# A two-block transformer forward pass: the low part of streamed weights made by an accumulating DMA instead of a GpSimd subtraction

## Chip, cores, metric

One NeuronCore of a Trainium2 chip runs the whole program in one launch. The metric is device microseconds of one execution. Times are compared as the median of several runs.

## What is computed

The reference chains two blocks in float32 over 512 tokens of width 1024. Only the first block is touched by the change:

```
h = x
h = h + token_mixer(rmsnorm(h))           # w_in (two attentions: top-k "A", differential "B"), w_out
h = h + cross_attention(rmsnorm(h), mem)  # w_xk, w_xv on 256 memory rows; w_xq, w_xo
h = h + conv_glu(rmsnorm(h))              # w_ffn_in, w_ffn_out
...
second_block(h)                           # gated recurrence, latent attention, merge, norm
```

Every `x @ w` is done to more than single-pass precision: an operand is written as a high part (rounded to the matmul's own format, fp32r) plus a low part (operand minus high part), and a product is three matmuls, high by high, high by low and low by high.

## The kernel before

**Weights.** A weight chunk is streamed from DRAM in pieces of 128 partitions by 1024 columns (512 KB). `W(src, nk, ncol)` (line 178) takes one buffer of the ring `WH` (high parts) and one of the ring `WL` (low parts) per piece, four buffers each, and calls `split` (line 167). `split` takes a raw buffer `WR` (ring of three), loads the piece with a DMA on SyncE's queue (line 169), writes the high part (line 173 on GpSimd, POOL, or line 175 on ScalarE, ACT) and subtracts it from the raw piece for the low part (line 176, on VectorE, DVE, or on POOL). A chunk of 8 k-tiles by 256 columns is two pieces, so the four buffers hold two chunks: one in use by TensorE (PE), one being prepared.

**Who does which part** is set by `setw`: the modes are taken in turn, the first letter naming the engine of the high part (`a` ACT, `p` POOL), the second that of the low part (`d` DVE, `p` POOL). From line 767 to line 1127 the mode is `"ap"`: ACT rounds, POOL subtracts. That stretch has 56 pieces: 16 of `w_inc` (projections of the token mixer), 8 each of `w_xk`, `w_xv`, `w_out`, `w_xq`, `w_xo`. It is the stretch from about 24 to 445 us of the span. Before it only the first projection (`w_in0`) is streamed, after it come the feed-forward part and the second block.

**Stages of that stretch.** Up to about 124 us PE runs the projections; DVE and POOL apply norms and rotary tables to their results (lines 392 to 430, 550) and DVE runs the index scores (line 808) and the top-k of attention A (lines 819, 822). From 124 to 200 us the first half of the differential attention runs (`soft`: line 609 maxima on DVE, line 617 exponentials on ACT). From 200 to 305 us its second half, attention A and the projections of the memory (lines 941 to 979) share the engines. From 305 us on, `residual_lin` (`w_out`), the query projections and cross-attention, and `w_xo` follow, with PE busy almost without a break.

**Order.** The program is written as interleaved generators (`pipeline`); a scheduler then sets the order of the instructions on each engine and each engine runs its own queue strictly in that order. An instruction that waits holds everything behind it on its engine. `mm3` (lines 218 to 220) issues the three matmuls of a product.

Of the kernel before, what the change touches and what calls it, by code (L numbers as in the profile page):

```python
# [14 lines left out]
AF = mybir.ActivationFunctionType  # L15
OP = mybir.AluOpType
# [46 lines left out]
def _body(nc, tc, ctx, d):  # L63
    TT = nc.vector.tensor_tensor
    TS = nc.vector.tensor_scalar
    STT = nc.vector.scalar_tensor_tensor
    ACT = nc.scalar.activation
    PTT = nc.gpsimd.tensor_tensor
# [43 lines left out]
    def rr(ap):  # L112
        return ap.bitcast(F32R)
# [7 lines left out]
    def f32(ap):  # L121
        return ap.bitcast(F32)
# [40 lines left out]
    def setw(*m):  # L163

        wmode[:], wturn[0] = m, 0

    def split(src, h, l, raw=None):
        raw = wr_()[:, :src.shape[-1]] if raw is None else raw
        nc.sync.dma_start(raw, src)
        m = wmode[wturn[0] % len(wmode)]  # L170
        wturn[0] += 1
        if m[0] == "p":
            PTS(h, raw, 1.0, 0.0, op0=OP.mult, op1=OP.add)  # L173
        else:
            ACT(h, raw, AF.Copy)  # L175
        (TT if m[1] == "d" else PTT)(l, raw, f32(h), op=OP.subtract)  # L176

    class W:


        def __init__(self, src, nk, ncol):
            self.per = 1024 // ncol
            self.hi, self.lo = [], []
            for k0 in range(0, nk, self.per):
                n = (min(nk, k0 + self.per) - k0) * ncol
                h, l = wh_(F32R)[:, :n], wl_(F32R)[:, :n]
                split(src[:, k0 * ncol:k0 * ncol + n], h, l)
                self.hi.append(r3(h, ncol))
                self.lo.append(r3(l, ncol))
# [20 lines left out]
    def steps(g, last):  # L210

        for st_ in g:
            if st_ == last:
                return True
        return False
# [110 lines left out]
    for k in range(KD):  # L326
        if k:
            nc.sync.dma_start(xs[k], d["xT"][:, k * T:(k + 1) * T])
        if k == 1:
            nc.scalar.dma_start(pos, d["pos"])  # L330
        if k % 2 == 0:
            raw, h, l = wr_(), wh_(F32R), wl_(F32R)
        c_ = slice((k % 2) * N0, (k % 2 + 1) * N0)
        split(d["w_in0"][:, k * N0:(k + 1) * N0], h[:, c_], l[:, c_], raw[:, c_])
        w0.append((h[:, c_], l[:, c_]))
        hilo(X.hk(k), X.lk(k), xs[k], v_("g_mix", k), pool=k % 2 == 1)
        st.add(xs[k])
# [426 lines left out]
    st0["tab_kk"] = kk  # L764
    st0["tab_i"] = (kk[0][:, :, 1:2], kk[1][:, :, 1:2])
    steps(proj, "end")
    setw("ap")
    steps(proj, "end")
    st0["tab_kb"] = rope_table([3], 1, tabs[2][:, :256], tabs[2][:, 256:])
    st0["tab_qb"] = rope_table([2], 1, tabs[3][:, :256], tabs[3][:, 256:])  # L770
# [83 lines left out]
    drain(proj)  # L854


    setw("ap")
    Oa = Act(4, R[0:1], R[1:2])
    banks(2, 2, 2, 2)
    poA, poB = Ring(pout.t[0:1]), Ring(pout.t[1:2])  # L860
# [870 lines left out]
    for q in range(4):  # L1731
        next(ma)
        h, l = (rr(t[q // 2][:, (q % 2) * 1024:(q % 2) * 1024 + 1024]) for t in (R[8:10], R[10:12]))
        split(d["w_o2"][0][:, q * 1024:(q + 1) * 1024], h, l)
        wo_hi += [h[:, 0:512], h[:, 512:1024]]
        wo_lo += [l[:, 0:512], l[:, 512:1024]]
# [3 lines left out]
    for n in range(NT):  # L1740
        s_ = slice(n * P, n * P + P)
        x = [xr(), xr()]
# [105 lines left out]
```

## Time and profile before

| | us |
|---|---|
| median of three runs | 1481.96 (1481.84 to 1483.73) |
| the profiled execution | 1483.48 |
| its span, first to last instruction | 1481.70 |
| PE busy | 1433.6 (97% of the span) |
| DVE busy | 967.2 (65%) |
| ACT busy | 571.5 (39%) |
| POOL busy | 504.2 (34%) |

Busy times are unions of the records on an engine. Issuing a DMA is not counted as busy. The ends of matmuls are modelled, so a busy PE is not PE at its peak. The granted clock is that of TensorE, 1.00 being 2.4 GHz and 0.50 being 1.2 GHz. A gap is put down to the semaphore that came last.

### The profile page before, as it was taken

What the parts mean: (1) busy time and instruction counts of PE and PEld (TensorE: products, weight loads), DVE (VectorE), ACT (ScalarE), POOL (GpSimd) and SP (SyncE); (2) the same over time, 40 slices, a digit from 0 to 9 for tenths busy, and PEclk for the clock granted to TensorE, in tenths of its full rate; (3) what the DMA queues carried; (4) which work ended last, traced back from release to release, by engine and by line L of the source; (5) the groups of instructions that cost most, each with busy time, mean ns of one, the idle gap of its engine ahead of it and who ended that gap; (6) DMA issues with size and microseconds to landing.
All of it is one profiled execution on the core that took longest, in us unless ns stands there. A gap on an engine that the chain in (4) does not pass through costs nothing.

```text
span 1481.7 us, 21172 instructions
## 1 busy us (share of the span) xinstructions
PE 1433.6 (97%) x7920; PEld 1240.7 (84%) x7920; DVE 967.2 (65%) x1908; ACT 571.5 (39%) x1136; POOL 504.2 (34%) x455
## 2 busy tenths in 40 slices
PE   6989899999999999999999999999999999998998
PEld 5988899888878788888888988888888898977887
DVE  8899898654445776356665556655448777886553
ACT  4535767744542222112223345344323333342121
POOL 6665677445531332332321111121114222331110
PEclk9999989999999999999999999999999999999999
DMA  6121143233212222333223422222332223235522
GB/s 213 59 72 58 44 143 123 92 108 134 72 58 86 100 89 76 98 122 100 87 78 106 129 90 92 86 93 82 133 110 79 100 97 111 79 121 189 196 78 86
DMA packets 54039, 150.59 MB, mean 102 GB/s; under 512 B 6064, under 2 KB 11696, under 8 KB 53936
## 3 DMA queue, kind: packets, MB, share of 16 engines
q1 hardware_dynamic: 53792, 149.24, 30.5%
q8 instruction: 62, 1.02, 0.3%
q14 instruction: 41, 0.34, 0.1%
q10 hardware_dynamic: 144, 0.00, 0.0%
HBM read 134.54 MB, written 14.68 MB: 101 GB/s over the span
## 4 chain that ended last, share of the span: by engine, by line
PE 81%; DVE 9%; issue 4%; ACT 2%; DMA 2%; POOL 1%; SPq 0%; POOLq 0%; DVEq 0%; ACTq 0%
PE PS L218 19%; PE PS L219 18%; PE PS L220 18%; PE PT L218 7%; PE PT L219 7%; PE PT L220 7%; PE PS L437 2%; DVE R L155 1%; PE PS L1400 1%; DVE WL L176 1%; DVE S L822 1%; DVE S L808 1%; PE PS L876 1%; DVE keep L819 0%; DMA S<-kv_d 0%
## 5 line engine op out<-in xcount | busy, mean ns | idle before, releaser
L218 PE MATMUL PS<-R,WH 128*128 128x512 f32 x920 | 359.1, 392 | 1.8 <-DVE S L1156 1.0
L219 PE MATMUL PS<-R,WH 128*128 128x512 f32 x920 | 359.5, 391 | 0.2 <-DVE R L155 0.2
L220 PE MATMUL PS<-R,WL 128*128 128x512 f32 x920 | 358.4, 391 | 0.0
L176 DVE TENSOR_TENSOR WL<-WR,WH 128x1024 fp32r<-128x1024 f32 (+4 forms) x176 | 209.7, 1194 | 110.2 <-ACT WH L175 91.2
L175 ACT ACTIVATE WH<-WR 128x1024 fp32r<-128x1024 f32 (+2 forms) x144 | 150.1, 1044 | 220.6 <-PE PS L219 151.6
L173 POOL TENSOR_SCALAR WH<-WR 128x1024 fp32r<-128x1024 f32 (+3 forms) x88 | 89.0, 1011 | 370.1 <-PE PS L219 145.6
L218 PEld LDWEIGHTS PS<-R,WH 128*128 128x128 f32 x920 | 172.5, 188 | 37.8 <-DVE S L1156 1.5
L220 PEld LDWEIGHTS PS<-R,WL 128*128 128x128 f32 x920 | 173.0, 188 | 35.7
L219 PEld LDWEIGHTS PS<-R,WH 128*128 128x128 f32 x920 | 173.1, 188 | 34.8 <-DVE R L155 0.5
L218 PE MATMUL PS<-WH,R 128*128 128x256 f32 (+2 forms) x568 | 166.8, 299 | 7.4 <-POOL WH L173 5.5
L220 PE MATMUL PS<-WH,R 128*128 128x256 f32 (+2 forms) x568 | 168.1, 297 | 1.5 <-DVE R L152 1.5
L176 POOL TENSOR_TENSOR WL<-WR,WH 128x1024 fp32r<-128x1024 f32 x56 | 139.5, 2500 | 86.7 <-ACT WH L175 77.9
L219 PE MATMUL PS<-WL,R 128*128 128x256 f32 (+2 forms) x568 | 166.7, 295 | 0.9 <-DVE WL L176 0.9
L218 PE MATMUL PT<-R,WH 128*128 128x512 f32 x352 | 140.4, 399 | 4.6 <-DVE S L1706 3.6
L219 PE MATMUL PT<-R,WH 128*128 128x512 f32 x352 | 139.7, 397 | 1.7 <-DVE R L155 1.7
L220 PE MATMUL PT<-R,WL 128*128 128x512 f32 x352 | 139.4, 396 | 0.0
L218 PEld LDWEIGHTS PS<-WH,R 128*128 128x128 f32 x568 | 111.6, 197 | 10.7 <-POOL WH L173 5.5
L220 PEld LDWEIGHTS PS<-WH,R 128*128 128x128 f32 x568 | 111.1, 196 | 4.6 <-DVE R L152 1.9
L219 PEld LDWEIGHTS PS<-WL,R 128*128 128x128 f32 x568 | 110.8, 195 | 4.6 <-DVE WL L176 2.3
L218 PEld LDWEIGHTS PT<-R,WH 128*128 128x128 f32 x352 | 67.4, 192 | 19.1 <-DVE S L1706 3.9
L219 PEld LDWEIGHTS PT<-R,WH 128*128 128x128 f32 x352 | 67.1, 191 | 15.5 <-DVE R L155 2.3
L220 PEld LDWEIGHTS PT<-R,WL 128*128 128x128 f32 x352 | 67.3, 191 | 14.3
(395 smaller groups left out, 2641.2 us busy)
## 6 DMA issues: line engine op xcount, KB each, us to landing
WR<-w_fi_d SPq DMA_DIRECT2D x44, 512.0 KB, 3.6
WR<-w_inc_d SPq DMA_DIRECT2D x16, 512.0 KB, 3.6
WR<-w_fo_d SPq DMA_DIRECT2D x16, 512.0 KB, 3.7
WR<-w_gl_d SPq DMA_DIRECT2D x16, 512.0 KB, 3.2
WR<-w_xk_d SPq DMA_DIRECT2D x8, 512.0 KB, 3.6
WR<-w_xv_d SPq DMA_DIRECT2D x8, 512.0 KB, 3.6
WR<-w_out_d SPq DMA_DIRECT2D x8, 512.0 KB, 3.6
WR<-w_xq_d SPq DMA_DIRECT2D x8, 512.0 KB, 3.6
```

The costliest lines, as they stand in the source:

```text
L155: TT(ol, src, f32(oh), op=OP.subtract)
L173: PTS(h, raw, 1.0, 0.0, op0=OP.mult, op1=OP.add)
L175: ACT(h, raw, AF.Copy)
L176: (TT if m[1] == "d" else PTT)(l, raw, f32(h), op=OP.subtract)
L218: nc.tensor.matmul(ps, sh, mh, start=first, stop=False)
L219: nc.tensor.matmul(ps, sh, ml, start=False, stop=False)
L220: nc.tensor.matmul(ps, sl, mh, start=False, stop=last)
L437: nc.tensor.transpose(out, in_, ident)
L808: STT(sc[b], rl, wi[:, b, h:h + 1], sc[b], op0=OP.mult, op1=OP.add)
L822: nc.vector.match_replace(sc[b], m8, sc[b], TAKEN)
L876: nc.tensor.matmul(ps, qa[g][:, q2 * 2 + hh, b * P:(b + 1) * P], rr(ka[j])[:, :N], start=j == 0, stop=j == 1)
L1400: nc.tensor.matmul(ps, qp[hh][:, s_], rr(kpe[j])[:, :N], start=False, stop=j == 1)
```

## The change

Mode `"ap"` becomes `"ax"` in both places. In this mode ACT writes the high part as before; ACT also writes minus the high part into the low-part buffer (the raw piece times -1, rounded to the same format); then a DMA on GpSimd's queue loads the same piece from DRAM a second time and adds it to what is in the buffer, which leaves raw minus high part there. The GpSimd subtraction is gone. All lines behind line 176 move down by five.

```diff
-        (TT if m[1] == "d" else PTT)(l, raw, f32(h), op=OP.subtract)
+        if m[1] == "x":
+
+            ACT(l, raw, AF.Copy, scale=-1.0)
+            nc.gpsimd.dma_start(l, src, accum_op=OP.add)
+        else:
+            (TT if m[1] == "d" else PTT)(l, raw, f32(h), op=OP.subtract)
...
-    setw("ap")
+    setw("ax")
...
-    setw("ap")
+    setw("ax")
```

The instructions of the engines move with it, since the scheduler orders them anew. Three places:

POOL's queue where the first pieces of `w_inc` are prepared (about 25 us), before. Names are out<-in, with buffer numbers:

```order
L151 TENSOR_SCALAR R_62<-S_96,vec 128x512
L176 TENSOR_TENSOR WL_105<-WR_99,WH_101 128x1024
L176 TENSOR_TENSOR WL_106<-WR_100,WH_102 128x1024
L176 TENSOR_TENSOR WL_107<-WR_98,WH_103 128x1024
L415 TENSOR_TENSOR S_82<-S_96,S_90 128x2x32
L416 TENSOR_TENSOR S_82<-S_96,S_90 128x2x32
```

The same place in the changed kernel:

```order
L151 TENSOR_SCALAR R_62<-S_96,vec 128x512
L179 DMA WL_105<-w_inc_d 128x1024
L179 DMA WL_106<-w_inc_d 128x1024
L179 DMA WL_107<-w_inc_d 128x1024
L420 TENSOR_TENSOR S_82<-S_96,S_90 128x2x32
L421 TENSOR_TENSOR S_82<-S_96,S_90 128x2x32
```

Three subtractions that read two buffers have become three DMA issues at the same place of the queue.

ACT's queue at the same time, before:

```order
L365 ACTIVATE S_83<-S_84 128x4x32
L175 ACTIVATE WH_101<-WR_99 128x1024
L175 ACTIVATE WH_102<-WR_100 128x1024
L175 ACTIVATE WH_103<-WR_98 128x1024
L490 ACTIVATE S_96<-PS_114 128x452
```

and in the changed kernel:

```order
L370 ACTIVATE S_83<-S_84 128x4x32
L175 ACTIVATE WH_101<-WR_99 128x1024
L178 ACTIVATE WL_105<-WR_99 128x1024
L175 ACTIVATE WH_102<-WR_100 128x1024
L178 ACTIVATE WL_106<-WR_100 128x1024
L178 ACTIVATE WL_107<-WR_98 128x1024
L175 ACTIVATE WH_103<-WR_98 128x1024
L495 ACTIVATE S_96<-PS_114 128x452
```

Each rounding has a second ACT instruction of the same shape beside it, from the third piece on ahead of it.

ACT's queue in the stretch from 200 us on, where the memory's key and value weights are prepared between exponentials (L617), before:

```order
L175 ACTIVATE WH_102<-WR_98 128x1024
L960 ACTIVATE S_90<-PS_110,SMALL 128x256 x2
L175 ACTIVATE WH_103<-WR_99 128x1024
L978 ACTIVATE S_92<-PS_111,keep 128x256 x2
L175 ACTIVATE WH_104<-WR_100 128x1024
L617 ACTIVATE S_97,keep<-S_97,SMALL,keep 128x384
L617 ACTIVATE S_83,SMALL<-S_83,SMALL,keep 128x128
L175 ACTIVATE WH_101<-WR_98 128x1024
```

and in the changed kernel (exponentials are L622 there):

```order
L965 ACTIVATE S_90<-PS_110,SMALL 128x256 x2
L178 ACTIVATE WL_107<-WR_99 128x1024
L175 ACTIVATE WH_103<-WR_99 128x1024
L178 ACTIVATE WL_108<-WR_100 128x1024
L983 ACTIVATE S_92<-PS_111,keep 128x256 x2
L175 ACTIVATE WH_104<-WR_100 128x1024
L622 ACTIVATE S_97,keep<-S_97,SMALL,keep 128x384
L622 ACTIVATE S_83,SMALL<-S_83,SMALL,keep 128x128
```

The exponentials now stand behind two ACT instructions per piece.

## Rows read from the trace of the kernel before

**Rows 1.** The page: busy time, share of the span and instructions of each engine; and the granted clock in 40 slices of the span, in tenths.
```profile
PE 1433.6 (97%) x7920; PEld 1240.7 (84%) x7920; DVE 967.2 (65%) x1908; ACT 571.5 (39%) x1136; POOL 504.2 (34%) x455
...
PEclk9999989999999999999999999999999999999999
```

**Rows 2.** Busy time of each engine in stretches of the span: stretch, its length, busy us and instructions of PE, PE's weight load, DVE, ACT and POOL, then granted clock, DMA share and GB/s.
```profile
core 0: us, PE busy (x) PEld busy (x) DVE busy (x) ACT busy (x) POOL busy (x), PEclk, DMA share, GB/s
24.00:124.00 100.00, 88.59 (x650) 83.47 (x650) 94.11 (x239) 46.83 (x96) 65.63 (x53) 0.97 0.24 78
...
174.00:200.00 26.00, 21.17 (x126) 17.51 (x126) 22.14 (x52) 19.58 (x44) 21.14 (x15) 0.80 0.36 110
200.00:280.00 80.00, 79.78 (x610) 74.72 (x608) 69.30 (x252) 62.94 (x173) 53.39 (x49) 1.00 0.38 126
...
305.00:331.00 26.00, 26.00 (x117) 21.52 (x116) 16.35 (x14) 12.90 (x18) 18.13 (x8) 1.00 0.32 99
331.00:445.00 114.00, 112.15 (x568) 93.72 (x567) 54.19 (x89) 53.62 (x101) 54.89 (x43) 1.00 0.26 89
```

**Rows 3.** Waits of PE from 24 to 124 us: who waited for whom, us in total, times, longest.
```profile
PE PS L287 <- DVE S L285: 3.5, 1, 3.5
PE PS L437 <- DVE F L418: 3.0, 2, 1.6
PE PS L441 <- DVE Q L550: 1.7, 1, 1.7
PE PS L437 <- ACT S L804: 1.6, 1, 1.6
PE PS L220 <- DVE R L155: 1.2, 1, 1.2
```

**Rows 4.** DVE in order of time (start us, duration us, line, operation, out<-in, shape): the first and the last of eleven long instructions, two between them, and short ones of the same line and shape.
```profile
25.42 0.28 DVE L395 TENSOR_TENSOR S<-S,S 128x128 f32<-128x128 f32 x1
...
26.49 2.90 DVE L152 SCALAR_TENSOR_TENSOR R<-S,vec,R 128x512 fp32r<-128x512 f32 x1
29.32 2.50 DVE L395 TENSOR_TENSOR S<-S,S 128x128 f32<-128x128 f32 x1
...
86.67 2.78 DVE L808 SCALAR_TENSOR_TENSOR S<-S,keep,S 128x512 f32<-128x512 f32 x1
...
89.97 0.73 DVE L808 SCALAR_TENSOR_TENSOR S<-S,keep,S 128x512 f32<-128x512 f32 x1
...
96.14 0.68 DVE L417 TENSOR_TENSOR F<-S,S 128x512 f32<-128x512 f32 x1
...
104.32 2.88 DVE L417 TENSOR_TENSOR S<-S,S 128x512 f32<-128x512 f32 x1
```

**Rows 5.** POOL in order of time: subtractions of line 176 (a row with x3 holds three, back to back).
```profile
25.40 8.61 POOL L176 TENSOR_TENSOR WL<-WR,WH 128x1024 fp32r<-128x1024 f32 x3 [6.54 <-ACT WH L175]
...
86.49 2.41 POOL L176 TENSOR_TENSOR WL<-WR,WH 128x1024 fp32r<-128x1024 f32 x1 [5.70 <-ACT WH L175]
...
101.48 5.17 POOL L176 TENSOR_TENSOR WL<-WR,WH 128x1024 fp32r<-128x1024 f32 x2
```

**Rows 6.** Groups of instructions from 24 to 445 us, shapes kept apart: line, engine, operation, count, busy us, mean ns, then idle time before them; and the busy time of line 175 alone on ACT from 200 to 280 us.
```profile
L176 POOL TENSOR_TENSOR WL<-WR,WH 128x1024 fp32r<-128x1024 f32 x56 | 139.5, 2500 | 86.7 <-ACT WH L175 77.9 <-issue 7.2 <-DMA WR<-w_xv_d 0.7
...
L175 ACT ACTIVATE WH<-WR 128x1024 fp32r<-128x1024 f32 x56 | 59.2, 1060 | 24.5 <-PE PS L219 14.2 <-PE PS L220 6.3 <-DMA WR<-w_inc_d 2.8
...
200.00:280.00 80.00, 14.84 (x14) 1.00 0.38 126
```

**Rows 7.** DMA: loads by name with count, KB each and median us from issue to landing; the issue of one load on SyncE's queue; landing times of all loads of line 169 from 0 to 450 us.
```profile
WR<-w_xk_d SPq DMA_DIRECT2D x8, 512.0 KB, 3.6
...
WR<-w_pb_d SPq DMA_DIRECT2D x8, 512.0 KB, 4.4
...
308.15 0.33 SPq L169 DMA_DIRECT2D WR<-w_xq_d  x1
...
DMA to landing us min/median/max: 3.2/3.6/6.1
```

**Rows 8.** Two low parts and the first matmul that reads each (which buffer it is follows from the order of the instructions): on POOL, then on PE, at 186 and at 311 us.
```profile
185.96 2.54 POOL L176 TENSOR_TENSOR WL<-WR,WH 128x1024 fp32r<-128x1024 f32 x1
...
189.93 0.56 PE L219 MATMUL PS<-WL,R 128*128 128x256 f32 x1
...
310.77 2.40 POOL L176 TENSOR_TENSOR WL<-WR,WH 128x1024 fp32r<-128x1024 f32 x1 [2.64 <-ACT WH L175]
...
317.54 0.39 PE L220 MATMUL PS<-R,WL 128*128 128x512 f32 x1
```

**Rows 9.** Around the PE pause at 182 us: a subtraction on POOL, the row behind it on POOL, the DVE instruction that ends with the subtraction, and PE's longest wait there.
```profile
175.11 2.54 POOL L176 TENSOR_TENSOR WL<-WR,WH 128x1024 fp32r<-128x1024 f32 x1 [3.31 <-ACT WH L175]
177.88 1.64 POOL L581 TENSOR_TENSOR keep<-SMALL,nhalf 128x8 f32<-128x8 f32 x1 [0.24 <-DVE SMALL L579]
...
175.30 2.37 DVE L579 TENSOR_SCALAR SMALL<-SMALL,keep 128x4 f32<-128x4 f32 x1
...
184.57 0.79 PE L218 MATMUL PS<-R,R 64*128 64x512 f32 x1 [2.72 <-DVE SMALL L609]
```

## The prediction, made before the changed kernel ran

> **What bounds the kernel now.** I read the page first: PE is busy 97% of the span, so only what shortens or lengthens PE's pauses, or its time at the lower clock, can move the end [rows 1]. The clock line shows where to look: nearly all slices are at full clock. Next the table of stretches, for the 421 us in which the change acts [rows 2]. Two stretches have PE pauses worth naming: 24 to 124 us, with PE idle 11.4 of 100 us, and 174 to 200 us, idle 4.8 of 26 us with a granted clock of 0.80. From 200 to 280 and from 305 us on PE is busy nearly throughout. In 24 to 124 us DVE is the fullest engine (94.1 of 100), and the list of PE's waits there puts 9.4 us on DVE, in four rows [rows 3].
>
> Then DVE in order of time. Eleven of its instructions between 26.5 and 107 us take 1.0 to 2.9 us where the same line and shape, or for one the nearest, takes 0.2 to 0.75 us elsewhere: L395 2.50 against 0.28, L808 2.78 against 0.73, L417 2.88 against 0.68 [rows 4]. POOL in order of time shows that each of them runs beside a subtraction of line 176 and ends with it: POOL's at 25.40, 86.49 and 101.48 us span the long ones at 26.49, 86.67 and 104.32 [rows 5]. Taking from each its ordinary duration leaves 21.9 us in all (2.2, 2.05 and 2.2 us for the three named). The GpSimd subtraction thus holds up the engine that PE waits for. The reader should see that POOL's own busy time is not the cost.
>
> **The change, part by part.** *Removed:* 56 subtractions of 2.50 us, 139.5 us of POOL [rows 6]. POOL is at 66% in 24 to 124 us and 67% in 200 to 280 us, so its time is free; what counts is the 21.9 us given back to DVE. DVE would then be busy 94.1 - 21.9 = 72.2 of 100 us, and PE with 88.6 is the fullest. The gain is at least 0 (another wait takes each pause) and at most the 11.4 us that PE is idle. I take 8 us, near the upper end, because 9.4 us of the waits name DVE itself and the first (3.5 us, L287 on L285) stands right behind three stretched instructions: **-8 us**.
>
> This needs the DMA's issue not to hold DVE in the same way. No row shows that; the bounds are no hold (all 21.9 us come back) and a hold as long as now (none do). I take no hold, since the issue moves no tensor through POOL. The Trainium skill, SBUF — State Buffer, section Who interferes with whom, says that a DVE instruction with two SBUF inputs collides with a GpSimd instruction that reads SBUF and not with one that only writes it; the trace agrees for the first half (L395, L808 and L417 have two inputs), and no run here yet shows the second.
>
> From 174 to 200 us the subtraction at 175.11 stretches DVE's L579 to 2.37 us, and POOL's L581, which needs L579, starts at 177.88, once both are done; PE pauses 2.72 us at 182 us at the end of that chain [rows 9]. Without it the chain is some 2 us earlier. Against that, PE reads the low part of 185.96 only 1.4 us after its end [rows 8], and the new way is later (below). I set **-0.5 us**; the bounds are -5 (pause and half-clock time both gone; 0.20 of 26 us is 5.2) and +4.
>
> *Added on ACT:* 56 instructions of the shape of line 175, 1.06 us each, 59 us [rows 6]. In 24 to 124 us ACT is at 47%: covered. From 305 us on it is at about 48%: covered. From 200 to 280 us it is busy 62.9 us, 14 roundings among them; 14 more make 62.9 + 14.8 = 77.7 of 80 us [rows 2, 6]. There the cover is gone: ACT becomes the fullest engine but for PE, its queue is strict, and behind each new instruction wait exponentials that PE needs. The stretch loses nothing if the instructions fall into ACT's gaps; if ACT does no better than 90%, half-way between the 79% it shows there now and all of the time, it lasts 77.7/0.9 = 86 us, 6 us more. I take the middle: **+3 us**.
>
> *Added on GpSimd's queue:* 56 DMAs of 512 KB. Issue: at least the 0.33 us of SyncE's queue [rows 7], at most the 2.50 us it replaces; I take 1 us, nearer the one other DMA issue in the trace. POOL has room for either. The rotary and normalisation steps behind the DMA now wait for ACT's second write, about 1 us later, but no longer for 2.4 us of subtraction.
>
> Landing: at least the 3.6 us of a plain load of that size; at most twice that, 7.2 us, since the DMA also reads what it adds to (the slowest plain load takes 6.1). I take 4.4 us, the row of loads that share the queues with others [rows 7], as these will. The Trainium skill, DMA: Bandwidth & Descriptors, section Anatomy of one DMA, gives 2.0 us plus the bytes at 436 GB/s for a DMA from GpSimd, 3.2 us as an estimate for 512 KB without the addition; with it instead of 4.4 us no term changes.
>
> So a low part that was ready 2.4 us after the high part is now ready 1.06 + 1 + 4.4 = 6.5 us after it, 4.1 us later (where ACT writes the negative first, 1 us less). Who notices? PE's first reading of a low part comes 4.4 us after the subtraction's end at the tightest place of the `w_out` stretch (313.17 to 317.54) and 1.4 us after it at 188.5 us [rows 8]. Before the first, 4.1 us just fit, with **+0.5 us** for the neighbours (0 to +4); the second is in the -0.5 us above.
>
> *Added traffic:* 56 x 512 KB, 29 MB. In the fullest stretch the DMA engines are at 0.38 [rows 2], and 14 more pieces add 7.3 MB to the 10 MB there, so share rises to about 0.66 without filling them: 0 us. SyncE's queue loses nothing: raw buffers come free when ACT has read them twice, earlier than after a subtraction.
>
> Sum: -8 - 0.5 + 3 + 0.5 = **-5 us** on the span of 1481.7 us. The profiled execution took 1483.48 us and the median of the runs is 1481.96, so the median should come to 1477.0 us. No change can be told from 0.2%, 3.0 us, and less.
>
> **The rivals.** *ACT takes it back* (no measurable change). DVE's relief brings only 5 us, since the pauses turn into waits for something else, and the full 6 us of the stretch from 200 us are lost: -5 + 6 = +1, 1483 us. For: 77.7 of 80 us. Against: from 200 to 280 us DVE loses stretches too, and POOL's normalisations no longer queue behind subtractions. Chance 0.18.
>
> *The accumulating DMA lands late* (slower). Its place is wherever PE reads a low part soon after it is made. Extra lateness is 1.06 + 1 + landing - 2.4 us; at 311 us it passes the 4.4 us slack when landing exceeds 4.8 us, and the other tight places (5 to 8 us of slack, by the same reckoning) follow from 5.4 us on. At 7.2 us a piece is 6.9 us later: 2.5 us late at 311, 5.5 us late at 188, and with two neighbours each of some 2 us about 12 us in all, so -8 + 12 + 3 = +7, **1489 us**. For: the addition reads two streams, and DMA share rises. Against: plain loads land in 3.6 us, and most low parts have 8 us and more. Chance 0.32, with ACT at its worst as the companion that makes the smaller losses of the kind.
>
> By a rule of the page on SBUF, section SBUF: two separate sides, a DMA issued from GpSimd cannot have its descriptors written while a DVE instruction in a two-port mode runs. As a mechanism here each issue would wait for one ordinary DVE instruction, up to 0.7 us [rows 4]; landing counts 0.7 us longer, which by itself costs under 1 us and is part of this case's chance. That rule is the Trainium skill's; no run here shows it yet.
>
> *The pauses go altogether* (faster). DVE runs 21.9 us ahead, and with it the 2.7 us pause at 182 us and the half-clock time around it disappear too: -10 - 5 + 3 = -12, 1470 us. For: DVE is at 94% up to 124 us and all that follows depends on it. Against: other engines' orders were made anew. Chance 0.15.
>
> **How the numbers follow.** The forecast (about -5 us, all results from -3 to -9) has 0.35; with the last rival, faster is 0.50, no change 0.18, slower 0.32. These are near one another because the gain rests on measured stretches but the price of the accumulating DMA on no row at all. The range takes in the rivals of both signs and leaves 0.2 outside: 1467 to 1490 us. The faster cases alone run from 1467 to 1479 us.
>
> **What would show it.** Right: no two-input DVE instruction over about 1 us from 24 to 124 us; DVE busy near 72 and PE over 93 of a stretch of some 92 us; the new ACT line at 1.06 us; the accumulating loads landing in 3.6 to 5 us; from 200 us on ACT at 95% or more and that stretch 3 us longer. Wrong: DVE still stretched beside the DMA issues; PE waiting for low parts that a DMA writes; landings over 5 us; PE pauses from 24 to 124 us that name ACT or DMA where DVE stood; the stretch from 200 us unchanged or longer by more than 6 us.

## The result, and the profile after

The changed kernel took 1497.36 us (median of four runs, 1496.20 to 1498.77); the kernel before, in the same session, 1482.85 us (1481.84 to 1485.06). The ratio is 1.0103, 95% interval 1.0086 to 1.0120: **15 us slower**, where 5 us faster was forecast and 1490 us was the end of the range.

The page, engines' busy time and the new DMA queue with packets, MB and share of 16 engines' span (before: [rows 1]):

```profile
PE 1439.8 (96%) x7920; PEld 1245.7 (83%) x7920; DVE 918.7 (61%) x1908; ACT 618.4 (41%) x1192; POOL 415.8 (28%) x455
...
q0 software_dynamic: 8064, 29.36, 10.7%
```

GpSimd and VectorE lost the work that they were to lose. Queue 0 is new: it holds the accumulating DMAs. The same stretches as in [rows 2], and one of 20 us inside them; columns as there:

```profile
24.00:124.00 100.00, 95.65 (x723) 90.91 (x721) 85.46 (x270) 65.47 (x123) 46.45 (x58) 0.97 0.66 157
...
174.00:200.00 26.00, 23.55 (x150) 21.46 (x150) 18.77 (x61) 20.32 (x43) 7.70 (x10) 0.75 0.78 182
200.00:280.00 80.00, 73.43 (x521) 67.87 (x520) 52.16 (x209) 64.91 (x165) 25.61 (x41) 0.94 0.82 206
...
331.00:445.00 114.00, 104.33 (x531) 86.68 (x530) 41.88 (x85) 63.21 (x111) 32.95 (x41) 1.00 0.62 145
...
200.00:220.00 20.00, 19.74 (x152) 18.20 (x151) 17.62 (x70) 19.02 (x47) 6.60 (x12) 1.00 1.04 269
```

Two halves tell against each other. Up to 124 us TensorE does 723 matmuls where it did 650. From 200 us it does 521 for 610, and from 331 us 531 for 568. The last row shows what the mean over 80 us hides: from 200 to 220 us the DMA engines are **full** (1.04; records that overlap count twice). A stretch at a fixed time is no stretch of the same work, though: TensorE comes to 200 us with a lead here, and the versions e_plain and e_noload below, both faster, do 518 and 531 matmuls from 200 to 280 us. So 521 for 610 doesn't by itself measure what the DMAs cost.

TensorE's waits from 24 to 445 us:

```profile
PE PS L225 <- DMA WL<-w_xq_d: 5.2, 2, 3.3
PE PS L224 <- DMA WL<-w_inc_d: 4.3, 1, 4.3
PE PS L224 <- DMA WL<-w_xv_d: 3.8, 1, 3.8
PE PS L224 <- DMA WL<-w_xk_d: 2.7, 2, 2.4
...
PE PS L225 <- DMA WL<-w_out_d: 1.9, 2, 1.1
```

All five name low parts that a DMA writes, 17.9 us together; in the kernel before no row of TensorE's waits in that time names a low part. One of them in order of time, on ACT, POOL and PE:

```profile
173.54 1.04 ACT L178 ACTIVATE WL<-WR 128x1024 fp32r<-128x1024 f32 x1
...
174.88 0.92 POOL L179 DMA_DIRECT2D WL<-w_xk_d  x1 [0.69 <-ACT S L717]
...
182.63 0.58 PE L224 MATMUL PS<-WL,R 128*128 128x256 f32 x1 [2.42 <-DMA WL<-w_xk_d]
```

The negative is written by 174.58 us, and TensorE reads the low part at 182.63 us, 8 us later and the moment it has landed. This is the place of the pause in [rows 9]: the subtraction that delayed it is gone, and a late DMA stands there.

Issue to landing up to 470 us (count, KB, median us; then the queues' shares in that time), and the least, middle and longest landing of the accumulating DMAs (before: [rows 7]):

```profile
q0 software_dynamic: 8064, 29.36, 34.2%
q1 hardware_dynamic: 15408, 44.10, 29.3%
...
WR<-w_inc_d SPq DMA_DIRECT2D x16, 512.0 KB, 7.9
WL<-w_inc_d POOLq DMA_DIRECT2D x16, 512.0 KB, 9.1
WR<-w_xk_d SPq DMA_DIRECT2D x8, 512.0 KB, 8.4
...
kv_d<-S SPq DMA_DIRECT2D x8, 256.0 KB, 7.8
...
DMA to landing us min/median/max: 5.5/8.6/12.4
```

The accumulating DMA lands after 8.6 us, and the plain raw loads beside it take 7.9 and 8.4 us where they took 3.6. The shares give the reason: 34.2% of 16 engines in 470 us, over 8,064 packets, is 319 ns each; queue 1 comes to 143 ns with its smaller packets among them. By the records of single 4 KB packets the medians are 327 ns for one that adds and 159 ns for a plain one on SyncE's queue over the whole execution (173 ns up to 470 us). That is about twice the time for the same bytes.

VectorE and POOL in order of time (as [rows 4] and [rows 5]):

```profile
30.06 0.28 DVE L400 TENSOR_TENSOR S<-S,S 128x128 f32<-128x128 f32 x1
...
80.00 2.78 DVE L813 SCALAR_TENSOR_TENSOR S<-S,keep,S 128x512 f32<-128x512 f32 x1
...
91.22 0.68 DVE L422 TENSOR_TENSOR S<-S,S 128x512 f32<-128x512 f32 x1
...
80.50 1.03 POOL L420 TENSOR_TENSOR S<-F,S 128x256 f32<-128x256 f32 x1
81.20 1.02 POOL L421 TENSOR_TENSOR S<-F,S 128x256 f32<-128x256 f32 x1
```

The stretched instructions are back at their ordinary length. The one that is left, at 80.00 us, runs beside two GpSimd instructions with two inputs that the change doesn't touch. Where only DMA issues run on GpSimd beside them, 33 two-input instructions of VectorE lose 0.2 us in all, so an issue doesn't hold VectorE as a subtraction did.

### The profile page after: what moved, and what is told of

It reads as the page before. It is cut to its first block, busy times and chain, and to the rows that moved or that the text cites. A ratio compares the mean times of both kernels' runs of the same rounds, so it can differ in the third digit from the quotient of the medians.

```text
span 1497.0 us, 21254 instructions
## 1 busy us (share of the span) xinstructions
PE 1439.8 (96%) x7920; PEld 1245.7 (83%) x7920; DVE 918.7 (61%) x1908; ACT 618.4 (41%) x1192; POOL 415.8 (28%) x455
## 3 DMA queue, kind: packets, MB, share of 16 engines
q0 software_dynamic: 8064, 29.36, 10.7%
## 4 chain that ended last, share of the span: by engine, by line
PE 79%; DMA 6%; DVE 4%; ACT 4%; issue 4%; POOL 1%; SPq 0%; POOLq 0%; DVEq 0%; ACTq 0%
PE PS L224 18%; PE PS L223 18%; PE PS L225 18%; PE PT L223 7%; PE PT L225 7%; PE PT L224 7%; PE PS L442 2%; DMA WR<-w_xq_d 1%; DMA WL<-w_xk_d 1%; ACT WL L178 1%; ACT WH L175 1%; DMA S<-kv_d 1%; DVE R L155 1%; PE PS L1405 1%; DVE WL L181 1%
## 5 line engine op out<-in xcount | busy, mean ns | idle before, releaser
L223 PEld LDWEIGHTS PS<-WH,R 128*128 128x128 f32 x568 | 112.2, 198 | 13.3 <-POOL WH L173 6.8
L154 ACT ACTIVATE R<-S 128x512 fp32r<-128x512 f32 x46 | 28.9, 631 | 123.6 <-DVE S L1161 44.5
```

The costliest lines, as they stand in the source:

```text
L154: ACT(oh, src, AF.Copy)
L223: nc.tensor.matmul(ps, sh, mh, start=first, stop=False)
```

## The experiments

Differences in us are ratios to the kernel before, times 1482; an interval of a ratio is 0.0009 to 0.0024 to either side, 1.3 to 3.5 us.

The scheduler orders the queues of each version anew. By the names and shapes in the traces, only e_plain has the changed kernel's order, on every engine. In the other versions that use mode `"ax"` throughout, 407 (e_half) to 1,092 (e_noload) of TensorE's 7,920 matmuls are others at the same place. What an order is worth was not measured, so a difference of a few us from these versions can be the order's.

**Halves of the change: e_first, e_second.** The mode is `"ax"` for one stage only, `"ap"` in the other.

```diff
 # e_first, second place        # e_second, first place
-    setw("ax")                 -    setw("ax")
+    setw("ap")                 +    setw("ap")
```

> The change is kept for the pieces of the first stage (the projection by w_inc, up to 124 us of the span), and the later pieces (w_xq, w_xk, w_xv, w_out, w_xo) get the GpSimd subtraction again. Theory A (the relief of VectorE up to 124 us is a real gain, and the accumulating DMAs of the later stages cost more than it): the 8 to 9 us that TensorE had lost less by 124 us stay, so -7 to -9 us on the kernel before, 1474 to 1476. Rival B (the relief only lets TensorE run ahead and it waits for the same later work): within 3 us of the kernel before, 1480 to 1486. Rival C (the accumulating DMA costs as much in the first stage, seen only later): slower than before, over 1486.

Measured: 1475.5 us, ratio 0.9948 (0.9933 to 0.9963), -7.7 us. TensorE in the first stretch, and its only wait there of over 0.1 us:

```profile
24.00:124.00 100.00, 97.50 (x734) 92.46 (x733) 86.36 (x271) 65.94 (x124) 46.41 (x58) 0.98 0.66 158
```

```profile
PE PS L224 <- DMA WL<-w_inc_d: 2.5, 1, 2.5
```

> The other half: GpSimd subtraction for the pieces of the first stage, negative write and accumulating DMA for all later ones. Theory A: the whole cost without the gain, +20 to +25 us on the kernel before, 1503 to 1508, with the waits of L225 and L224 on DMA-written low parts all after 124 us. Rival B (no gain in the first stage): about the changed kernel's +14 us, 1495 to 1499. Rival C (half of the cost sits in the first stage): +5 to +10 us, 1488 to 1493.

Measured: 1510.9 us, ratio 1.0190 (1.0167 to 1.0214), +28 us. Theory A holds in sign and place: the first stage alone gains what was forecast for it, the later stages lose. The loss is above A's 20 to 25 us; without the first stage's lead TensorE arrives later, but that this makes the difference to the 23 us between 1.0103 and 0.9948 isn't shown.

**Which part of the new way costs: e_noload, e_plain.**

```diff
 # e_noload
-            nc.gpsimd.dma_start(l, src, accum_op=OP.add)
 # e_plain
-            nc.gpsimd.dma_start(l, src, accum_op=OP.add)
+            nc.gpsimd.dma_start(l, src.bitcast(F32R))
```

> The accumulating DMA is left out and everything else of the change is kept: ScalarE still writes the negative of the raw piece into the low part (so the low part lacks the addition of the raw piece). Theory 1 (the DMA, by its late landing or its traffic, is the cost): TensorE's waits on DMA-written low parts and the late raw loads both go, the gain up to 124 us stays, 1468 to 1475. Rival 3 (ScalarE's 56 more writes are the cost): no better than 1490. Rival 4 (the new order of the engines' queues): 1482 to 1497, with pauses that name neither.

Measured: 1469.8 us, ratio 0.9913 (0.9898 to 0.9928), -13 us. Theory 1 holds. ScalarE does all the added writes here, and from 200 to 280 us is busier than in the changed kernel (68.5 us for 64.9):

```profile
24.00:124.00 100.00, 99.56 (x761) 93.82 (x760) 88.05 (x287) 69.29 (x142) 36.73 (x46) 1.00 0.26 83
...
200.00:280.00 80.00, 73.84 (x531) 67.17 (x531) 55.20 (x219) 68.47 (x183) 19.90 (x34) 0.98 0.27 94
```

So ScalarE's writes don't make the loss; with the DMA the time is 0.0190, 28 us, longer. Rival 4 isn't settled by this version, since its queues have an order of their own; e_plain, next, settles it.

> The second load stays on GpSimd's queue with its 512 KB, and only the addition is taken from it (the low part becomes the raw piece itself, with the same rounding to the float32r type). Theory 1a (the addition in the DMA is what is slow; its packets take 327 ns where plain ones take 159): packets near 160 ns, second loads land in 4 to 5.5 us, raw loads back to 4 to 5.5, time 1476 to 1486. Rival 1b (two loads of 512 KB at once fill the engines, whatever they do): second loads and raw loads land in 7 to 9 us as in the changed kernel, time 1493 to 1500. Rival 1c (GpSimd's queue itself is slow): second loads land in 7 to 9 us with raw loads back near 4, time 1486 to 1495.

Measured: 1479.4 us, ratio 0.9980 (0.9968 to 0.9992), -3 us. The same table of DMA:

```profile
q0 software_dynamic: 8064, 29.36, 19.6%
...
WR<-w_inc_d SPq DMA_DIRECT2D x16, 512.0 KB, 5.2
WL<-w_inc_d POOLq DMA_DIRECT2D x16, 512.0 KB, 5.2
```

A packet takes 183 ns by the share (median of single 4 KB packets 174). Theory 1a holds. With the changed kernel's order on every engine, all of ScalarE's writes and all of the bytes, but no addition, the kernel is 3 us faster than before. So rival 4 falls too: the addition alone makes it 18 us slower. (To e_noload it is 10 us, but there the order differs as well. The issue takes GpSimd 0.55 to 0.60 us without the addition and 0.87 to 0.91 us with it, medians by tensor.)

Since the order is the same, the two traces can be laid side by side, matmul by matmul. Groups of rows: the issue on POOL, and the matmul that reads the low part (which issue belongs to it follows from landing time and order). The issue at 174.88 us and its matmul are shown above. The changed kernel, in the second group with a wait of ScalarE just before:

```profile
26.58 1.06 POOL L179 DMA_DIRECT2D WL<-w_inc_d  x1 [7.71 <-DVE S L399]
35.85 0.58 PE L224 MATMUL PS<-WL,R 128*128 128x256 f32 x1 [4.35 <-DMA WL<-w_inc_d]
...
334.83 1.06 ACT L175 ACTIVATE WH<-WR 128x1024 fp32r<-128x1024 f32 x1 [3.90 <-DMA WR<-w_xq_d]
339.04 0.86 POOL L179 DMA_DIRECT2D WL<-w_xq_d  x1 [1.02 <-ACT WL L178]
349.01 0.50 PE L225 MATMUL PS<-R,WL 128*128 128x512 f32 x1 [3.29 <-DMA WL<-w_xq_d]
```

and e_plain, with its row for 200 to 280 us at the end:

```profile
26.67 0.76 POOL L179 DMA_DIRECT2D WL<-w_inc_d  x1 [7.71 <-DVE S L399]
33.34 0.39 PE L224 MATMUL PS<-WL,R 128*128 128x256 f32 x1 [1.74 <-DMA WL<-w_inc_d]
...
170.29 0.64 POOL L179 DMA_DIRECT2D WL<-w_xk_d  x1 [0.78 <-ACT S L717]
175.70 0.58 PE L224 MATMUL PS<-WL,R 128*128 128x256 f32 x1
...
326.54 0.53 POOL L179 DMA_DIRECT2D WL<-w_xq_d  x1 [1.33 <-ACT WL L178]
334.22 0.39 PE L225 MATMUL PS<-R,WL 128*128 128x512 f32 x1
...
200.00:280.00 80.00, 73.69 (x518) 67.80 (x517) 52.61 (x212) 65.55 (x172) 22.83 (x41) 0.94 0.53 175
```

The first DMA is issued at the same time in both, 26.6 us, and lands 9.2 us later with the addition and 6.6 us later without it; TensorE starts the matmul behind it 2.5 us later. In the changed kernel its granted clock is then 0.64 from 36 to 42 us (1.00 in e_plain from 34 to 38 us), and the lag grows to 4.5 us. In the changed kernel's time it is 7.6 us at 190 us, 8.8 us at 322 us and 18.2 us at 373 us, and it stays there up to 445 us. At eight waits for low parts it grows by 14.0 us of the 18.2; the rest comes at the lower clock behind them and in shorter waits. At six of the eight the DMA is issued no later than the lag that is there already, at the other two, behind ScalarE's waits of 3.5 and 3.9 us for a raw piece, 1.0 and 1.2 us later; from issue to landing each takes 0.9 to 3.4 us longer than its counterpart. So the price of the addition comes to TensorE mainly through the longer landing, and only in small part (2.2 us) through raw loads that make the issue late. The stretch from 200 to 280 us, where the DMA engines are full, adds only about 1 us.

**What in the addition: e_half, e_sbuf.**

```diff
 # e_half
-            nc.gpsimd.dma_start(l, src, accum_op=OP.add)
+            w = src.shape[-1] // 2
+            nc.gpsimd.dma_start(l[:, :w], src[:, :w], accum_op=OP.add)
 # e_sbuf
-            nc.gpsimd.dma_start(l, src, accum_op=OP.add)
+            nc.gpsimd.dma_start(l, raw, accum_op=OP.add)
```

> The accumulating DMA adds the raw piece to the left half of the columns alone (the right half of each low part lacks the addition); all else is the change. Measured so far: 1469.8 us without the DMA, 1479.4 with a full-size one that doesn't add, 1497.4 with the full-size one that adds. Theory E (the cost follows the time that the packets hold the DMA engines): packets of 2 KB at 160 to 180 ns, about those of the full-size plain load, landing 5 to 6 us, so 1476 to 1483. Rival F (an accumulating DMA costs its delay whatever its size): landing over 7 us, 1488 to 1497.

Measured: 1486.9 us, ratio 1.0031 (1.0018 to 1.0044). Between the two expectations, a miss for both; the packets are as E has them, 178 ns for 2 KB, the landing a little later:

```profile
q0 software_dynamic: 8064, 14.68, 19.2%
...
WL<-w_inc_d POOLq DMA_DIRECT2D x16, 256.0 KB, 6.2
```

Engine time equal to that of e_plain (19.2 and 19.6%) costs 7.6 us more here, and the landing is 1 us longer (6.2 for 5.2 us). Engine time is thus not the whole cost, as far as the two orders can be compared.

> The accumulating DMA reads the raw piece from its SBUF buffer instead of a second time from HBM (the result is that of the change); the raw buffer is held until the DMA has landed. Theory E (the engines' work on the addition is the cost, not where the source lies): packets at 300 ns or more, landing 7 to 9 us, time 1493 to 1503. Rival H (the second read from HBM is the cost): packets near 175 ns, landing under 6 us, 1476 to 1488.

Measured: 1503.7 us, ratio 1.0136 (1.0115 to 1.0157). A packet from SBUF to SBUF takes as long as one from HBM (median of single packets 339 ns):

```profile
q0 software_dynamic: 8064, 29.36, 34.5%
...
WL<-WR POOLq DMA_DIRECT2D x56, 512.0 KB, 5.3
```

Theory E holds on packets, 1503.7 us is just outside its range (1493 to 1503), and Rival H falls on both; so the addition matters and not where the source lies. The landing (7 to 9 us expected) was missed. That the raw buffers, which are held meanwhile, cost what the shorter landing saves is likely from e_mirror's rows below, but not shown. The Trainium skill, Collectives: The Full Stack, section The bandwidth ceiling, says of the DMA engines' adding in another setting that it isn't the sum that costs but the second source read, which halves the rate; 327 against 174 ns agrees with a half.

**Late low part, or crowded engines: e_halfscr, e_mirror, e_accraw, e_store2, e_tiny.** The first three give the traffic to a buffer that TensorE doesn't read. All five edits take the place of the same accumulating DMA; the lines that set up the scratch buffers are left out here.

```diff
 # e_halfscr (scr: one tile of 512 columns)
-            nc.gpsimd.dma_start(l, src, accum_op=OP.add)
+            w = src.shape[-1] // 2
+            nc.gpsimd.dma_start(rr(scr[:, :w]), src[:, :w], accum_op=OP.add)
 # e_mirror
+            nc.gpsimd.dma_start(rr(raw), f32(l), accum_op=OP.add)
 # e_accraw
+            nc.gpsimd.dma_start(rr(raw), src, accum_op=OP.add)
 # e_store2
+            for _ in range(2):
+                nc.gpsimd.dma_start(d["scr"][stn[0]][:, :l.shape[-1]], f32(l))
+                stn[0] += 1
 # e_tiny
+            nc.gpsimd.dma_start(l[:, :32], src[:, :32], accum_op=OP.add)
```

> The same half-size accumulating DMA, but into a 2 KB scratch tile that nobody reads, so that low parts are complete (as the negative alone, without the addition) once ScalarE has written them: the traffic without the wait for it. Theory L (TensorE's wait for the late low part is most of the cost): the time is that without the DMA, 1469 to 1473, 4 us or more under the half-size one into the low part. Rival T (the traffic itself, which delays the raw loads and the stores and loads of kv_d): within 3 us of the half-size one into the low part. What each DMA waits for here is the one before it on the scratch tile; pieces follow each other at 6 us, so this should hold GpSimd for a microsecond or two at times and no engine that is full.

Measured: 1546.1 us, ratio 1.0429 (1.0410 to 1.0449). It answers another question. Its scratch tile made each DMA wait for the one before, in GpSimd's strict queue; two of six such rows of POOL's waits:

```profile
POOL SCR L182 <- DMA SCR<-w_xq_d: 29.7, 7, 6.3
POOL SCR L182 <- DMA SCR<-w_inc_d: 29.6, 13, 3.7
```

The six come to 137 us, and TensorE then waits for GpSimd's other work (its two longest rows, 18.8 us, name POOL). The expectation that this holds no full engine was the error: POOL isn't full, but what stands behind the wait is needed.

> The counterpart of the version whose accumulating DMA reads the raw buffer in SBUF (1503.7 us): the same 512 KB from SBUF to SBUF, at the same place and after the same two writes of ScalarE, but in the other direction, from the low part into the raw buffer, which nobody reads any more. The raw buffer is held as long as there, the packets are the same, only TensorE need not wait for them (the low part is the negative alone, without the addition). Theory L (TensorE's wait for late low parts, and the lower clock after it, is most of the cost): 1472 to 1482. Rival T (the traffic, and the raw loads that it makes late, is most of it): 1492 to 1504. About half-way, 1486 to 1490: each has a half.

Measured: 1501.2 us, ratio 1.0122 (1.0105 to 1.0139).

> As the changed kernel (1497.4 us), with its second read from HBM and its addition, but into the raw buffer after ScalarE has read it twice, so that no low part waits for the DMA (it is the negative alone, without the addition); the raw buffers come free later by the landing. Theory L: 1472 to 1482. Rival T: 1490 to 1500, with ScalarE's waits on raw loads as long as in the changed kernel or longer.

Measured: 1517.8 us, ratio 1.0231 (1.0207 to 1.0255). Both times fall on rival T's side (e_accraw above its range): no low part waits for a DMA here and the time is no better. But they don't measure the traffic alone, so they don't decide against Theory L. SyncE's queue and ScalarE in e_mirror:

```profile
SPq L169 <- DMA WR<-WL: 282.3, 49, 14.6
```

```profile
ACT WH L175 <- DMA WR<-w_xq_d: 11.0, 2, 10.7
```

Loads are issued late because the DMA still holds the raw buffer, so both parts of the weight come late. That is a price that the changed kernel doesn't have. Hence the next two.

> Traffic without anybody who needs it: in place of the accumulating DMA, GpSimd's queue stores each low part (the negative, without the addition) twice, 512 KB each, to scratch memory in HBM, after ScalarE has written it. Two plain packets of 4 KB at about 170 ns hold an engine as long as one that adds (327 ns). TensorE waits for neither, raw buffers come free as early as in the change, and only the next user of the low part's buffer waits for the stores. Theory L (TensorE's direct wait for late low parts is the cost of the DMA, 27.6 us between 1469.8 and 1497.4): 1469 to 1476. Rival T (the engines' time taken from the raw loads and from kv_d is the cost): 1488 to 1500, with raw loads landing in 7 to 8 us. Both a half: 1479 to 1486.

Measured: 1482.3 us, ratio 1.0008 (0.9999 to 1.0018). Packets at 159 ns, two for one:

```profile
q0 software_dynamic: 16128, 58.73, 31.7%
...
WR<-w_xk_d SPq DMA_DIRECT2D x8, 512.0 KB, 6.8
```

```profile
ACT WH L176 <- DMA WR<-w_xq_d: 12.1, 3, 4.6
```

That is 0.0095, 14 us, over none, where the expectation has "both a half". ScalarE waits 20.0 us for raw pieces here, 3.8 us in e_noload and 18.3 us in the changed kernel, so traffic that nobody needs can cost time by late raw loads. But the 14 us are not the traffic's part of the changed kernel's loss: this order is another, there are two issues a piece, and beside e_plain the changed kernel's late raw loads made a DMA's issue later by 1.0 and 1.2 us at two of eight waits only.

> The accumulating DMA is kept in place and order, but adds 32 of up to 1024 columns (the rest of the low part lacks the addition): the wait for an issue and a landing, without traffic. Together with none (1469.8), half (1486.9) and all of it (1497.4) it gives the cost by size. Theory L: a landing near 3 us makes the low part 2.5 us later than the subtraction did, less than the 4.4 us of slack of the tightest place but one: 1469 to 1473. If the fixed part of such a DMA (its issue on GpSimd, its landing without bytes) is a large share of the cost: 1476 to 1484.

Measured: 1476.3 us, ratio 0.9966 (0.9952 to 0.9980), 8 us over none. It lands later than the 3 us expected:

```profile
WR<-w_xk_d SPq DMA_DIRECT2D x8, 512.0 KB, 4.0
WL<-w_xk_d POOLq DMA_DIRECT2D x8, 16.0 KB, 4.5
```

A wait almost without bytes has a price too, and TensorE's rows name only 1.9 us of it as waits for low parts. Where the rest of the 8 us goes isn't settled; the two orders differ here too.

**Less of it: e_firstmix, e_mixall.**

```diff
 # both, first place; e_mixall in the second place too, e_firstmix "ap" there
-    setw("ax")
+    setw("ax", "ap")
```

> As the version that keeps the change for the first stage only, with every other piece of that stage given back to the GpSimd subtraction. Measured so far for the whole first stage: 1475.5, 6.8 us under the kernel before. If the relief is in proportion to the subtractions taken away: about half, 1478 to 1480. If the accumulating DMAs crowd one another in that stage (landing 8.7 us, TensorE waits 2.5 us for one) and half of the relief is enough for TensorE: 1472 to 1475.

Measured: 1473.6 us, ratio 0.9935 (0.9919 to 0.9951), -9.6 us: the fastest kernel here with the reference's computation. Half of the relief is enough; from e_first it can't be told apart (the intervals overlap). That half is enough speaks for the second expectation, though TensorE still waits 3.1 us there for one low part.

> The change for every other piece in all stages, GpSimd subtraction for the others (the result is that of the change). With every other piece of the first stage alone: 1473.6. If the later stages' cost goes with the number of accumulating DMAs: half of the 21 us that lie between 1475.5 and 1497.4 come on top, 1482 to 1486. If it comes from DMAs that crowd one another (their packets take 327 ns, and each piece's two loads hold an engine for 8 times 486 ns): under a quarter of it, 1473 to 1479, since with half of them landing falls from 8 to 6.5 us or less.

Measured: 1483.2 us, ratio 1.0007 (0.9993 to 1.0021): 10.7 us over e_firstmix. Its median lies in the first expectation's range, half the DMAs for half the cost; landing stayed at 7.6 to 9.0 us in the later stages, so thinning them out hardly made each faster.

## Why the prediction was wrong

**Landing at 4.4 us, bounds 3.6 to 7.2: the step that failed.** It was taken from rows of plain loads, and the upper bound was twice a plain load that runs by itself. Measured: 8.6 us, 5.5 to 12.4, since a packet that adds holds its engine for 327 ns and not about 170, while the raw load beside it wants the same engines. Without the addition the same DMA, in the same order, landed after 5.5 us, and the kernel was 3 us faster than before, where 5 had been forecast; with the addition it was 18 us slower than that. Both the packet and the load beside it count: in e_sbuf, whose raw loads often have to wait for it, a DMA with packets of 339 ns landed after 5.3 us. By the prediction's own formula a landing of 8.6 us makes a low part 1.06 + 1 + 8.6 - 2.4 = 8.3 us later, where 4.4 us of slack was the tightest but one. The rival "the accumulating DMA lands late" was the right one, with the right mechanism. At 7.2 us it had 12 us for the waits; measured are 18 us, at a longer landing and in more places than it had. Most of them are in the terms that follow.

**No term for late low parts up to 124 us.** The prediction looked for tight readers at 188 and 311 us only. TensorE's first wait for a DMA, 4.3 us at 35.85 us, is in neither place, and beside e_plain it costs 4.5 us with the lower clock behind it.

**-0.5 us from 174 to 200 us (-5 to +4):** can't be read off against the kernel before, since TensorE does other work there by then (150 matmuls for 126). Beside e_plain the addition costs 3 us there: the pause of [rows 9] has a new cause, the DMA of 174.88 us. The granted clock is 0.75; before it was 0.80.

**+0.5 us for the stretches from 305 us on (0 to +4):** too small; beside e_plain it is 9 us. TensorE is busy 104.3 of 114 us from 331 us, for 112.2; the longest wait is 3.3 us on `w_xq`, and the granted clock stays at 1.00 there, so this is all waiting.

**Traffic at 0 us: failed as a step, and part of the reason for the long landing.** "Share rises to about 0.66 without filling them" was a sum of bytes. In the stretch it was made for, 200 to 280 us, the share is 0.82 and reaches 1.04. "SyncE's queue loses nothing" went with it: a raw load takes 5.1 to 8.4 us (medians by tensor) instead of 3.6. What this alone cost is not isolated. Beside e_plain, whose raw loads take 4.2 to 5.6 us, it reached TensorE as 1.0 and 1.2 us at two places; against no second load at all it isn't known, since e_noload and e_store2 have other orders.

**-8 us up to 124 us: right as far as it goes.** e_first gives -7.7 us, the long instructions went, and the issue doesn't hold VectorE. But -7.7 us is what is left beside a wait of 2.5 us for a DMA, which the sum didn't have, so the agreement in size is in part luck. VectorE's busy time (72 of 100 us expected) was 85.5, in part since more work runs in the same 100 us (270 instructions for 239). Of long instructions the trace before shows twelve, not eleven; their excess, 21.8 us, is as stated.

**+3 us for ScalarE: not what happened.** It was busy 64.9 of 80 us, not 77.7, and e_plain and e_noload are faster than before with all its writes. Whether a few us of ScalarE are left in them wasn't tried.

The sum by the runs: -13 us without the DMA (e_noload), +10 us for a second load that doesn't add (e_plain), +18 us for the addition: +15 us. Only the last step keeps the order of the queues, so the -13 and the +10 are not shown to be those of the parts alone; their sum, -3 us, is that of the changed kernel without the addition.

## What to carry to other kernels

Price a DMA by the time its packets hold the DMA engines, not by its bytes: one that adds held them about twice as long here, and the loads beside it landed later too. Before a ready buffer is made later, list the slack of each of its readers, in every stage, and set it against the landing beside other loads. To price one part of a change, use a version that keeps the order of every queue, as e_plain does; then the traces can be compared instruction by instruction, and the place where the time goes shows itself. Where one change has a relief and a price in different stages, apply it by stage: here the first stage alone, even every other piece of it, beats both kernels.

## What the runs showed of the hardware

- An accumulating DMA took 327 ns for a 4 KB packet from HBM and 339 ns from SBUF, against 174 ns for the same DMA without the addition and 159 ns for a plain one on SyncE's queue. Beside the raw loads the one that adds landed after 8.6 us, the one that doesn't after 5.5 us (medians, 512 KB).
- An accumulating DMA of 16 KB still took 3.6 to 4.5 us (medians by tensor) to land.
- The issue of an accumulating DMA took GpSimd 0.87 to 0.91 us (medians by tensor), of a plain one 0.55 to 0.60 us. VectorE's two-input instructions beside the accumulating one kept their length, while one beside two-input GpSimd work took 2.78 us for 0.74.
